# Strassen products in two-bank PSUM tiles, each moved by one operation over both halves, the last sum's copy in place

## The chip, the cores and the metric

The kernel runs on one core of one Trainium2 chip. The metric is the device time of one execution in microseconds. A core has a matrix engine (TensorE, PE in the profile, with PEld for its weight loads), VectorE (DVE), ScalarE (ACT), GpSimd (POOL) and SyncE (SP), each with its own queue of instructions, worked off in order. TensorE writes its results to PSUM, an accumulator memory of eight banks, each of 512 float32 columns on 128 partitions; VectorE and ScalarE read them from there into SBUF, the working memory. DMAs move data between SBUF and the main memory.

## The reference

One layer of a hybrid decoder for a prompt of 1024 tokens and 8 sample tokens, width 1024, all in float32:

```python
h = rmsnorm(x, norm_gain)
proj = h @ w_in
q, k, v, gla_g, a_lr, u, pool_g, xq, xg, merge = jnp.split(proj, split_pts, axis=-1)
...
br_gla = o * jax.nn.silu(gla_g)          # gated linear attention
br_pool = p * jax.nn.silu(pool_g)        # trailing-window means, a map per group
br_x = c * jax.nn.silu(xg)               # cross-attention into 256 memory tokens
branches = jnp.stack([br_gla, br_pool, br_x], axis=2)
bproj = jnp.einsum('btnw,nwd->btnd', branches, w_branch)
gates = jax.nn.sigmoid(merge.astype(jnp.float32)).reshape(B, T, N_BRANCH, D_MODEL)
merged = jnp.sum(gates * bproj.astype(jnp.float32), axis=2).astype(x.dtype)
y = merged @ w_out
return x + y, S.astype(x.dtype), new_hist
```

A final RMSNorm follows. The change touches the product `h @ w_in`: 1024 rows of weights by some 10000 columns, for 1032 tokens.

## The kernel before

**Precision.** A float32 product is made of three: each operand is split into a rounded part (hi, a copy on ScalarE) and the rest (lo, a subtraction on VectorE, both in `split`, lines 219 to 226), and `mm3` (239 to 243) issues hi by hi, hi by lo and lo by hi. So TensorE's work stands under lines 241, 242 and 243 whatever it computes.

**Strassen.** The input projection is cut into 40 pairs of 128 columns each (`pairs`, 325 to 334; numbered 0 to 39). For one pair the 2x2 block product of weights and tokens is made with seven products in place of eight (Winograd's form): 0 to 6, with the left operands a11, a12, s2, s1, s3, s4 and a22 and the right ones in `ops`. One product has 128 output rows and 516 token columns; they are computed in two halves of 258 columns (QT), c = 0 and 1, each in a PSUM bank of its own, each with 4 x 3 = 12 matmuls (`product`, 536 to 544). Partial sums are shared by accumulating in PSUM: the tile x takes products 0, 2, 4 and 6 in turn, y takes 1, z takes 3 and then 5. In between, a snapshot of x is copied to SBUF on ScalarE (`saved`, 551 to 554): r1 after product 0, r2 after 2, r3 after 4. VectorE makes the sums: y + r1 (line 611), z + r3 (628) and z + r2 (637); what x holds after product 6 is copied out as it is (645, with SiLU, or 647). These sums go to the tiles e1 and e2, get a SiLU in 12 of the pairs (28 to 39, the gated ones), and are stored by a DMA of POOL (`finish`, 565 to 587).

**Order on TensorE.** It is written out by hand, as is that of SyncE, which issues the loads. `seq` (337 to 342) puts product 0 of the next pair between products 4 and 5 of this one:

```python
    for i in range(NPAIR):
        seq += [(i, j) for j in range(1, 5)]
        if i + 1 < NPAIR:
            seq.append((i + 1, 0))
        seq += [(i, 5), (i, 6)]
```

Pair 39, the last, has no next one. After each half of a product, `fill` (1239 to 1246) may put a piece of other work on TensorE: the memory keys and values, cross-attention, the linear attention, the pooling, each as a stream of steps with costs that set when the next one is due. These use two PSUM banks, the tag pz. The Strassen tiles, the first transposes of the tokens (`quarter_transposed`), the branch projections (1411 to 1436) and the output projection (1461 to 1506) use six, the tag px.

**Order elsewhere.** On ScalarE, VectorE and POOL the order is made by a planner with a cost model, which follows the program's order where several instructions are ready. It hands out the slots of a tag too, and sets the waits: a matmul that writes a bank waits for the last operation that read it.

**Buffers that the change touches.** `PX` (96) gives one bank, six in all. `Q` (130) gives an SBUF tile of 258 columns, five in all, for r1, r2, r3 and, early on, for the results of the memory stage (`mkv`, 405 to 413), which two POOL DMAs each store (456 and 457).

Of the kernel before, what the change touches and what calls it, by code (L numbers as in the profile page):

```python
# [9 lines left out]
F32 = mybir.dt.float32  # L10
# [8 lines left out]
P = 128  # L19
# [7 lines left out]
DV = 256  # L27
# [20 lines left out]
def trunk_kernel(ctx: ExitStack, tc: tile.TileContext,  # L48
# [44 lines left out]
    ps = ctx.enter_context(tc.tile_pool(name="ps", bufs=1, space=bass.MemoryType.PSUM))  # L93
    ctx.enter_context(tc.manual_schedule(engines={nc.tensor.engine, nc.sync.engine}))

    def PX():
        return ps.tile([P, 512], F32, tag="px", name="px", bufs=6)

    def PZ():
        return ps.tile([P, 512], F32, tag="pz", name="pz", bufs=2)  # L100
# [27 lines left out]
        return wk.tile([P, 4, P], dt, tag="w2", name=name, bufs=8)  # L128

    def Q(name):  # L130
        return wk.tile([P, QT], F32, tag="q", name=name, bufs=5)

    def tiny(w, name="t", bufs=8):
        return wk.tile([P, 16], F32, tag="t", name=name, bufs=bufs)[:, :w]
# [255 lines left out]
    def mem_units():  # L390
        loads = [mem_weights(0)]
        yield
        loads.append(mem_weights(1))
        yield
        for n in range(NH):
            h, o = divmod(n, 2)
            raw = loads.pop(0)
            if 0 < n < NH - 1:
                loads.append(mem_weights(n + 1))
            for a in range(2):  # L400
                t = PZ()
                for k in range(NK):
                    nc.tensor.matmul(t[:, :DV], lhsT=memT[k // 2][:, k % 2, a * P:(a + 1) * P],  # L403
                                     rhs=raw[k // 2][:, k % 2], start=k == 0, stop=k == NK - 1)
                m = Q("mkv")[:, :DV]
                if n + a == 0:
                    nc.vector.tensor_copy(m, t[:, :DV])
                elif n == 0:
                    with tc.issue_after(last["sc"].ins):
                        nc.vector.tensor_copy(m, t[:, :DV])  # L410
                else:
                    nc.scalar.activation(m, t[:, :DV], AF.Copy)
                mem_stored(h, o, a, m)
                yield

        steps = [(o, k) for o in range(2) for k in range(NK)]
        ahead = []

        def stream():
            o, k = steps[len(ahead)]  # L420
            ahead.append(loaded((w_mk, w_mv)[o][k * P:(k + 1) * P, 512:], [512], "wms", V))

        memr = []
        memT_done.append(True)
        for k2, x in enumerate(memT):
            memr.append(split_r(x, [2, NM], "memT"))
            if k2 % 2:
                stream()
            if k2 == 1:
                yield  # L430
        parts = {k: split_r(ahead[k], [512], "wms") for k in range(2)}
        stream()
        yield
        for n, (o, k) in enumerate(steps):
            if k == 0:
                ts = [PZ() for _ in range(2)]
            if len(ahead) < len(steps):
                stream()
            if n + 2 < len(steps):
                parts[n + 2] = split_r(ahead[n + 2], [512], "wms")  # L440
            wh, wl = parts.pop(n)
            for a in range(2):
                mh, ml = (x[:, k % 2, a * P:(a + 1) * P] for x in memr[k // 2])
                mm3(ts[a], mh, ml, wh, wl, k == 0, k == NK - 1)
            if k == NK - 1:
                for a in range(2):
                    m = V([2, DV], name="mkv")
                    nc.scalar.activation(m, ts[a].rearrange("p (h v) -> p h v", h=2), AF.Copy)
                    for h in range(2):
                        mem_stored(2 + h, o, a, m[:, h])  # L450
                if o == 0:
                    yield
            yield
# [82 lines left out]
    def product(acc, n, start):  # L536
        i, j = seq[n]
        lh, ll = left[i, j]
        for c in range(2):
            for k in range(4):  # L540
                hi, lo = ops[RIGHT[j]][k // 2]
                rh, rl = (x[:, k % 2, c * QT:(c + 1) * QT] for x in (hi, lo))
                mm3(acc[c][:, :QT], lh[:, k, :], ll[:, k, :], rh, rl, start and k == 0, k == 3, not start)
            yield c

    def run_product(n):
# [1 line left out]
        i, j = seq[n]  # L548
        p = pairs[i]

        def saved(acc, c, name):
            r = Q(name)
            nc.scalar.activation(r, acc[c][:, :QT], AF.Copy)  # L553
            return r

        def piece(t, h, c):
            return t[:, h, c * QT:(c + 1) * QT]

        def diagonal(x, e):

# [28 lines left out]
        def gate(t, h):  # L589
            if p.gated:  # L590
                act(t[:, h], t[:, h], AF.Silu)
# [7 lines left out]
                    p.mix[e].append(loaded(mix_scr[n][g][:, ch, 512 * hf:512 * hf + 512], [512], "mix"))  # L599

        if j == 0:
            p.x = [PX() for _ in range(2)]
            p.r1, p.mix = [], ([], [])
            for c in product(p.x, n, True):
                p.r1.append(saved(p.x, c, "r1"))
                yield
        elif j == 1:
            y = [PX() for _ in range(2)]
            p.e1 = E([2, HT], name="c1")
            for c in product(y, n, True):  # L610
                nc.vector.tensor_tensor(piece(p.e1, 0, c), y[c][:, :QT], p.r1[c], op=ALU.add)
                if c:
                    gate(p.e1, 0)
                yield
        elif j == 2:
            p.r2 = []
            for c in product(p.x, n, False):
                p.r2.append(saved(p.x, c, "r2"))
                yield
        elif j == 3:  # L620
            p.z = [PX() for _ in range(2)]
            mixed(0)
            for c in product(p.z, n, True):
                yield
        elif j == 4:
            for c in product(p.x, n, False):
                r3 = saved(p.x, c, "r3")
                nc.vector.tensor_tensor(piece(p.e1, 1, c), p.z[c][:, :QT], r3, op=ALU.add)  # L628
                if c:
                    gate(p.e1, 1)  # L630
                    finish(p.e1, 0)
                yield
        elif j == 5:
            p.e2 = E([2, HT], name="c2")
            mixed(1)
            for c in product(p.z, n, False):
                nc.vector.tensor_tensor(piece(p.e2, 0, c), p.z[c][:, :QT], p.r2[c], op=ALU.add)
                if c:
                    gate(p.e2, 0)
                yield  # L640
        else:
            for c in product(p.x, n, False):
                dst = piece(p.e2, 1, c)
                if p.gated:
                    act(dst, p.x[c][:, :QT], AF.Silu)
                else:
                    nc.scalar.activation(dst, p.x[c][:, :QT], AF.Copy)
                if c:
                    finish(p.e2, 1)
                yield  # L650

# [745 lines left out]
    def w_out_unit(k, hf):  # L1397
# [10 lines left out]
        split(hi, lo, raw)  # L1408
        wo[k, hf] = hi, lo

    for u, (o, n, d) in enumerate(units):
        if d == 0 and o:
            br = [branch_k(n, k) for k in range(NK)]
        if u + 1 < len(units):
            fetch(u + 1)
        w, sig, acc = inputs.pop(u)
        act(sig, sig, AF.Sigmoid)
        ts = [PX() for _ in CH]
        for k in range(NK):
            lh, ll = (x[:, k % 4, :] for x in w[k // 4])  # L1420
            for t, (c0, cw) in zip(ts, CH):
                mm3(t[:, :cw], lh, ll, br[k][0][:, c0:c0 + cw], br[k][1][:, c0:c0 + cw], k == 0, k == NK - 1)
        for t, (c0, cw) in zip(ts, CH):
            cs = slice(c0, c0 + cw)
            nc.vector.tensor_tensor(sig[:, cs], t[:, :cw], sig[:, cs], op=ALU.mult)
            if o > 0:
                nc.vector.tensor_tensor(sig[:, cs], acc[:, cs], sig[:, cs], op=ALU.add)
        if o < 2:
            nc.gpsimd.dma_start(out=acc_scr[o][d], in_=sig)
        else:  # L1430
            if d < 5:
                mg_split(d, sig)
            else:
                late.append((d, sig))
            if d >= 2:
                w_out_unit(d - 2, 0)
# [29 lines left out]
            mm3(t[:, :b - a], th, tl, wh, wl, k == 0, k == NK - 1)  # L1466


    begun = [PX() for _ in range(2)]
    for ks in (range(5), range(5, NK)):  # L1470
        for tb in range(2):
            row_block(begun[tb], tb, 0, 0, 512, ks)
    for hf, order in enumerate(ORDERS):
        for tb in order:
            m = P if tb < 8 else NS
            if tb >= 8:

                if tb == 8:
                    ts = PX()
                for j in range(4):  # L1480
                    nc.tensor.matmul(ts[32 * j:32 * j + 32], lhsT=mgs[:, 4 * (tb - 8) + j], rhs=own.pop(0),
                                     start=tb == 8, stop=tb == 9)
                if 2 * hf + tb < 11:
                    own_weights(2 * hf + tb - 7)
                if tb == 8:
                    continue
                tb = 8
# [9 lines left out]
                nc.vector.tensor_tensor(yl[:, :512], x[:, :512], fg[:, :512], op=ALU.mult)  # L1497
            n, a = hf, 0
            for b in ends:
                t = ts if tb == 8 else begun.pop(0) if begun else PX()  # L1500
                cs = slice(512 * hf + a, 512 * hf + b)
                if tb < 8 and (hf or tb > 1):
                    row_block(t, tb, hf, a, b, range(NK))
# [57 lines left out]
```

## Time and profile before

| what | us |
| --- | --- |
| median of 3 runs | 1450.72 |
| lowest and highest | 1450.0 and 1452.0 |
| the profiled execution | 1452.08 |
| its span | 1450.2 |
| TensorE busy | 1421.7 |
| VectorE busy | 906.0 |
| ScalarE busy | 689.2 |
| GpSimd busy | 194.9 |

The span is the time from the first to the last instruction that the profile shows; the execution's own time has the launch around it. The granted TensorE clock was 0.999 of full speed. The 40 pairs fill the first three quarters (to about 1079 us), the branch projections the next part, the output projection the end. In rows of the trace, the numbers are the start in us, the duration in us, the engine, the line, the operation, the tile written, the tiles read, and the shapes; what stands in brackets is idle time of the engine before the instruction and what ended it. In rows of one line's instructions three durations in ns follow: the shortest, the median and the longest. In rows of stretches, the wall time comes first and then each engine's busy time, with its count.

### The profile page before, as it was taken

The page shows a single profiled execution, that of the slowest core. Times are in us where ns is not written, and L with a number is a line of the kernel's source. Part 1 is how long each engine was busy: PE and PEld are TensorE (multiplying, and loading weights), DVE is VectorE, ACT ScalarE, POOL GpSimd, SP SyncE. Part 2 cuts the span into 40 slices and gives each one's busy share as a digit, 9 for nine tenths or more (in the row PEclk, how much of TensorE's full clock was granted, in tenths as well). Part 3 has the DMA queues.
Part 4 walks back from the last instruction along what each step waited for, and adds up shares of the span by engine and source line. Part 5 has one row for each costly group of instructions (what it writes and reads, how often), then busy time and mean ns, then how long its engine had stood idle before and what let it go on. Part 6 is the DMA issues. An engine that isn't in the chain of part 4 may idle for free.

```text
span 1450.2 us, 28260 instructions
## 1 busy us (share of the span) xinstructions
PE 1421.7 (98%) x10753; PEld 1360.2 (94%) x10753; DVE 906.0 (62%) x2107; ACT 689.2 (48%) x1607; POOL 194.9 (13%) x353
## 2 busy tenths in 40 slices
PE   7999999998999999999999999999999999999998
PEld 6899999998899999999999999999999999999876
DVE  6956656666686767766756678785672434544436
ACT  6744435443465666656654445454472333233312
POOL 3112101124341111111111111110010000000000
PEclk9999999999999999999999999999999999999999
DMA  9346665666655453553544455455594677632633
GB/s 335 122 159 207 200 212 184 218 190 164 160 157 183 130 182 126 177 175 125 180 142 152 157 187 182 138 192 168 194 303 147 226 255 236 241 116 71 220 125 117
DMA packets 182739, 259.42 MB, mean 179 GB/s; under 512 B 21436, under 2 KB 131796, under 8 KB 182596
## 3 DMA queue, kind: packets, MB, share of 16 engines
q1 hardware_dynamic: 159900, 183.87, 41.4%
q0 software_dynamic: 22560, 73.56, 14.1%
q8 instruction: 84, 1.38, 0.4%
q14 instruction: 51, 0.42, 0.1%
q10 hardware_dynamic: 144, 0.20, 0.0%
HBM read 180.47 MB, written 77.56 MB: 178 GB/s over the span
## 4 chain that ended last, share of the span: by engine, by line
PE 86%; DMA 5%; DVE 5%; issue 2%; ACT 1%; SPq 0%; DVEq 0%; POOL 0%; ACTq 0%
PE px L241 25%; PE px L242 24%; PE px L243 24%; DMA qb<-xqs 2%; PE pz L243 2%; PE pz L242 2%; PE pz L241 2%; DMA raw<-in_w_in_dram 2%; DVE kc L769 1%; PE pz L403 1%; PE pz L955 1%; PE pz L936 1%; PE pz L809 1%; PE pz L938 1%; DVE ws L304 0%
## 5 line engine op out<-in xcount | busy, mean ns | idle before, releaser
L243 PE MATMUL px<-bh,wbl 128*128 128x384 f32 (+1 forms) x576 | 184.1, 320 | 0.0
L242 PE MATMUL px<-bl,wbh 128*128 128x384 f32 (+1 forms) x576 | 184.1, 320 | 0.0
L241 PE MATMUL px<-bh,wbh 128*128 128x384 f32 (+1 forms) x576 | 183.7, 319 | 0.0
L553 ACT ACTIVATE r<-px 128x258 f32<-128x258 f32 x240 | 90.0, 376 | 45.6 <-PE px L243 45.0
L241 PEld LDWEIGHTS px<-bh,wbh 128*128 128x128 f32 x576 | 108.3, 188 | 0.0
L242 PEld LDWEIGHTS px<-bl,wbh 128*128 128x128 f32 x576 | 108.2, 188 | 0.0
L243 PEld LDWEIGHTS px<-bh,wbl 128*128 128x128 f32 x576 | 108.2, 188 | 0.0
L241 PE MATMUL px<-ot,s1h 128*128 128x258 f32 x320 | 93.9, 293 | 0.0
L241 PE MATMUL px<-ot,s3h 128*128 128x258 f32 x320 | 93.4, 292 | 0.0
L241 PE MATMUL px<-o,s4h 128*128 128x258 f32 x320 | 93.2, 291 | 0.2 <-DVE c L628 0.2
L241 PE MATMUL px<-o,a11h 128*128 128x258 f32 x320 | 92.9, 290 | 0.0
L241 PE MATMUL px<-o,a12h 128*128 128x258 f32 x320 | 92.9, 290 | 0.0
L241 PE MATMUL px<-ot,a22h 128*128 128x258 f32 x320 | 92.9, 290 | 0.0
L241 PE MATMUL px<-ot,s2h 128*128 128x258 f32 x320 | 92.3, 288 | 0.0
L242 PE MATMUL px<-o,a11h 128*128 128x258 f32 x320 | 91.0, 284 | 0.3 <-DVE o L223 0.3
L243 PE MATMUL px<-o,a11l 128*128 128x258 f32 x320 | 90.6, 283 | 0.0
L242 PE MATMUL px<-ot,a22h 128*128 128x258 f32 x320 | 90.5, 283 | 0.0
L242 PE MATMUL px<-ot,s2h 128*128 128x258 f32 x320 | 90.0, 281 | 0.5 <-DVE ot L223 0.5
L243 PE MATMUL px<-ot,s3l 128*128 128x258 f32 x320 | 90.5, 283 | 0.0
L243 PE MATMUL px<-o,a12l 128*128 128x258 f32 x320 | 90.4, 283 | 0.0
L242 PE MATMUL px<-o,a12h 128*128 128x258 f32 x320 | 90.4, 283 | 0.0
L243 PE MATMUL px<-ot,s1l 128*128 128x258 f32 x320 | 90.4, 282 | 0.0
(470 smaller groups left out, 4616.0 us busy)
## 6 DMA issues: line engine op xcount, KB each, us to landing
raw<-in_w_in_dram SPq DMA_DIRECT2D x80, 512.0 KB, 4.0
msc<-c POOLq DMA_DIRECT2D x24, 516.0 KB, 4.3
brsc<-c POOLq DMA_DIRECT2D x24, 516.0 KB, 4.0
sig<-msc SPq DMA_DIRECT2D x24, 516.0 KB, 6.6
mix<-mixsc SPq DMA_DIRECT2D x48, 256.0 KB, 4.5
brr<-brsc SPq DMA_DIRECT2D x48, 256.0 KB, 5.2
wbr<-in_w_branch_dram SPq DMA_DIRECT2D x24, 512.0 KB, 6.1
acc<-sig POOLq DMA_DIRECT2D x16, 516.0 KB, 5.3
```

The source lines that it names most:

```text
L241: nc.tensor.matmul(out, lhsT=lh, rhs=rh, start=start, stop=False, skip_group_check=more)
L242: nc.tensor.matmul(out, lhsT=lh, rhs=rl, start=False, stop=False, skip_group_check=more)
L243: nc.tensor.matmul(out, lhsT=ll, rhs=rh, start=False, stop=stop, skip_group_check=more)
L403: nc.tensor.matmul(t[:, :DV], lhsT=memT[k // 2][:, k % 2, a * P:(a + 1) * P], rhs=raw[k // 2][:, k % 2], start=k == 0, stop=k == NK - 1)
L553: nc.scalar.activation(r, acc[c][:, :QT], AF.Copy)
L769: nc.vector.tensor_tensor_reduce(kc[:, a, :], kc[:, a, :], qb[:, bb, :], scale=1.0, scalar=0.0, op0=ALU.mult, op1=ALU.add, accum_out=sc[:, ...
L809: nc.tensor.matmul(t[32 * j:32 * j + 32, :DV], lhsT=pm[:, a, 4 * i + j, :], rhs=vc[j][:, a, :], start=a == 0, stop=a == 1)
L936: nc.tensor.matmul(t[0:64, 0:P], lhsT=ki[:, 0:64], rhs=qi, start=True, stop=True)
L938: nc.tensor.transpose(t[:, P:2 * P], kt, ident)
L955: nc.tensor.matmul(to, lhsT=kiqi[:, 1, cs], rhs=st, start=False, stop=True)
```

## The change

Each Strassen tile becomes one tile of two banks (`PX2`, three of them), and half c is accumulated in bank c as before. Copies and sums are no longer made per half: after the second half, one operation over both banks does it, with the two halves of 258 columns as a second dimension. The snapshots r1 and r2 get two-half slots, two in all, in place of five single ones. The third snapshot, r3, gets none: ScalarE writes it to the place in e1 where the sum will be, and VectorE adds z to it there. The product after which an operation is made, the matmuls and their order, and the DMAs are the same.

Users of single banks are adapted: `PX` hands out the halves of a two-bank tile in turn, the memory results take halves of a two-half slot (`MKV`), and the projections at the end take three two-bank tiles once and go round their six banks.

```diff
+    def PX2():
+        return ps.tile([P, 2, 512], F32, tag="px", name="px", bufs=3)
+
+    banks = []
+
     def PX():
-        return ps.tile([P, 512], F32, tag="px", name="px", bufs=6)
+        if not banks:
+            t = PX2()
+            banks.extend([t[:, 0], t[:, 1]])
+        return banks.pop(0)
+
+    def banks_of(ts):
+        while True:
+            yield from (t[:, i] for t in ts for i in range(2))
...
     def Q(name):
-        return wk.tile([P, QT], F32, tag="q", name=name, bufs=5)
+        return wk.tile([P, 2, QT], F32, tag="q", name=name, bufs=2)
+
+    halves = []
+
+    def MKV():
+        if not halves:
+            q = Q("mkv")
+            halves.extend(q[:, i, :DV] for i in range(2))
+        return halves.pop(0)
...
-                m = Q("mkv")[:, :DV]
+                m = MKV()
...
-                mm3(acc[c][:, :QT], lh[:, k, :], ll[:, k, :], rh, rl, start and k == 0, k == 3, not start)
+                mm3(acc[:, c, :QT], lh[:, k, :], ll[:, k, :], rh, rl, start and k == 0, k == 3, not start)
...
-        def saved(acc, c, name):
+        def saved(acc, name):
             r = Q(name)
-            nc.scalar.activation(r, acc[c][:, :QT], AF.Copy)
+            nc.scalar.activation(r, acc[:, :, :QT], AF.Copy)
             return r
 
-        def piece(t, h, c):
-            return t[:, h, c * QT:(c + 1) * QT]
+        def half(t, h):
+            return t[:, h].rearrange("p (c q) -> p c q", c=2)
...
             for c in product(p.x, n, True):
-                p.r1.append(saved(p.x, c, "r1"))
+                if c:
+                    p.r1 = saved(p.x, "r1")
                 yield
...
             for c in product(y, n, True):
-                nc.vector.tensor_tensor(piece(p.e1, 0, c), y[c][:, :QT], p.r1[c], op=ALU.add)
                 if c:
+                    nc.vector.tensor_tensor(half(p.e1, 0), y[:, :, :QT], p.r1, op=ALU.add)
                     gate(p.e1, 0)
                 yield
...
             for c in product(p.x, n, False):
-                r3 = saved(p.x, c, "r3")
-                nc.vector.tensor_tensor(piece(p.e1, 1, c), p.z[c][:, :QT], r3, op=ALU.add)
                 if c:
+                    nc.scalar.activation(half(p.e1, 1), p.x[:, :, :QT], AF.Copy)
+                    nc.vector.tensor_tensor(half(p.e1, 1), p.z[:, :, :QT], half(p.e1, 1), op=ALU.add)
                     gate(p.e1, 1)
                     finish(p.e1, 0)
                 yield
...
             for c in product(p.z, n, False):
-                nc.vector.tensor_tensor(piece(p.e2, 0, c), p.z[c][:, :QT], p.r2[c], op=ALU.add)
                 if c:
+                    nc.vector.tensor_tensor(half(p.e2, 0), p.z[:, :, :QT], p.r2, op=ALU.add)
                     gate(p.e2, 0)
                 yield
...
             for c in product(p.x, n, False):
-                dst = piece(p.e2, 1, c)
-                if p.gated:
-                    act(dst, p.x[c][:, :QT], AF.Silu)
-                else:
-                    nc.scalar.activation(dst, p.x[c][:, :QT], AF.Copy)
                 if c:
+                    if p.gated:
+                        act(half(p.e2, 1), p.x[:, :, :QT], AF.Silu)
+                    else:
+                        nc.scalar.activation(half(p.e2, 1), p.x[:, :, :QT], AF.Copy)
                     finish(p.e2, 1)
                 yield
...
+    bank = banks_of([PX2() for _ in range(3)])
...
-        ts = [PX() for _ in CH]
+        ts = [next(bank) for _ in CH]
...
-    begun = [PX() for _ in range(2)]
+    begun = [next(bank) for _ in range(2)]
```

Product 2's copy (r2) and the tiles x, y and z change in the same way as those shown; in the output projection each remaining `PX()` becomes `next(bank)`.

More of the change, by code (lines that the diff above doesn't have):

```diff
@@ L601, in run_product @@
         if j == 0:
-            p.x = [PX() for _ in range(2)]
-            p.r1, p.mix = [], ([], [])
+            p.x = PX2()
+            p.mix = ([], [])
             for c in product(p.x, n, True):
-                p.r1.append(saved(p.x, c, "r1"))
+                if c:
+                    p.r1 = saved(p.x, "r1")
                 yield
         elif j == 1:
-            y = [PX() for _ in range(2)]
+            y = PX2()
             p.e1 = E([2, HT], name="c1")
             for c in product(y, n, True):
-                nc.vector.tensor_tensor(piece(p.e1, 0, c), y[c][:, :QT], p.r1[c], op=ALU.add)
                 if c:
+                    nc.vector.tensor_tensor(half(p.e1, 0), y[:, :, :QT], p.r1, op=ALU.add)
                     gate(p.e1, 0)
@@ L615, in run_product @@
         elif j == 2:
-            p.r2 = []
             for c in product(p.x, n, False):
-                p.r2.append(saved(p.x, c, "r2"))
+                if c:
+                    p.r2 = saved(p.x, "r2")
                 yield
         elif j == 3:
-            p.z = [PX() for _ in range(2)]
+            p.z = PX2()
             mixed(0)
@@ L1478, in trunk_kernel @@
                 if tb == 8:
-                    ts = PX()
+                    ts = next(bank)
                 for j in range(4):
@@ L1499, in trunk_kernel @@
             for b in ends:
-                t = ts if tb == 8 else begun.pop(0) if begun else PX()
+                t = ts if tb == 8 else begun.pop(0) if begun else next(bank)
                 cs = slice(512 * hf + a, 512 * hf + b)
```

## The prediction

> **What bounds the kernel now.** I read the profile page first: which engine is busy, and where the chain of waits that ends last runs.
>
> ```profile
> PE 1421.7 (98%) x10753; PEld 1360.2 (94%) x10753; DVE 906.0 (62%) x2107; ACT 689.2 (48%) x1607; POOL 194.9 (13%) x353
> PE 86%; DMA 5%; DVE 5%; issue 2%; ACT 1%; SPq 0%; DVEq 0%; POOL 0%; ACTq 0%
> ```
>
> TensorE is busy for 1421.7 us of the 1450.2 us span and carries 86% of the chain. So work taken from ScalarE (ACT) or VectorE (DVE) pays only where TensorE stands still for it, and at most 28.5 us stand still in all. Next, the stretches (wall, then busy time per engine) and the waits of TensorE, to see where that is.
>
> ```profile
> 300.00:600.00 300.00, 291.66 (x2408) 276.81 (x2407) 207.66 (x545) 170.35 (x458) 72.87 (x120) 1.00 0.55 164
> 780.00:1000.00 220.00, 220.00 (x1844) 219.77 (x1844) 158.77 (x349) 104.70 (x223) 26.83 (x47) 1.00 0.52 167
> 1100.00:1400.00 300.00, 300.00 (x1813) 288.73 (x1812) 129.49 (x243) 89.97 (x150) 10.81 (x23) 1.00 0.57 187
> ```
>
> ```profile
> PE px L241 <- DVE c L628: 0.2, 1, 0.2
> ```
>
> From 780 us on there is nothing to win: 220.00 of 220.00 us busy, then 300.00 of 300.00. From 300 to 600 us 8.3 us are idle. And among the waits of TensorE, one alone is for the operations that the change merges: 0.2 us, once. The evacuations are hidden today. The question is whether they stay hidden when they start later and last longer.
>
> **What the merging saves.** These are the prices: the two ScalarE rows read PSUM with 258 and with 512 columns, and the two VectorE rows do the same.
>
> ```profile
> L553 ACT ACTIVATE r<-px x240: 358/370/417, 28.7 to 1072.4; 128x258 f32<-128x258 f32 x120
> L448 ACT ACTIVATE mkv<-pz x4: 591/598/599, 85.9 to 110.5; 128x512 f32<-128x512 f32 x4
> L628 DVE TENSOR_TENSOR c<-px,r x80: 400/420/429, 71.5 to 1073.1; 128x258 f32<-128x258 f32 x80
> L503 DVE TENSOR_TENSOR h<-px,vec x7: 669/680/693, 21.2 to 46.5; 128x512 f32<-128x512 f32 x7
> ```
>
> A 516-column operation is not in the trace. Its bounds are the 512-column row (0.598 and 0.680 us) and two 258-column ones (0.740 and 0.840 us); with the slope between the rows I take 0.60 us on ScalarE and 0.68 us on VectorE, the near end. Each of the 40 pairs has four ScalarE copies per half (products 0, 2, 4, 6) and three VectorE adds per half (1, 4, 5). So 320 copies become 160, at 2 x 0.370 - 0.60 = 0.14 us saved each, 22 us of ScalarE; 240 adds become 120, at 2 x 0.420 - 0.68 = 0.16 us each, 19 us of VectorE. That is 3% and 2% of what these engines do, none of it on the chain.
>
> What it gives TensorE is unknown. The bounds are 0 and the whole 8.3 us idle between 300 and 600 us; most of that idle time waits for DMAs and for long steps of the attention chain, and so lies near the low end. I take an eighth, -1.0 us.
>
> **What it delays: a pair in the steady state.** A merged operation can't start before the second half of its product is done, and its reader gives both banks back at once. The tightest case is product 4: copy on ScalarE, add on VectorE, and product 5 accumulates onto the same tile z, with one product (0 of the next pair) between. Here is pair 36: the last matmul of product 4, what ScalarE and VectorE do, the first matmul of product 5.
>
> ```profile
> 1011.27 0.28 PE L243 MATMUL px<-ot,s3l 128*128 128x258 f32 x1
> ...
> 1014.28 0.28 PE L241 MATMUL px<-o,s4h 128*128 128x258 f32 x1
> ```
>
> ```profile
> 1011.51 0.63 ACT L222 ACTIVATE a12h<-raw 128x512 fp32r<-128x512 f32 x1 [0.98 <-PE px L242]
> 1012.05 0.37 ACT L553 ACTIVATE r<-px 128x258 f32<-128x258 f32 x1
> ```
>
> ```profile
> 1012.18 0.69 DVE L223 TENSOR_TENSOR a12l<-raw,a12h 128x512 fp32r<-128x512 f32 x1 [1.19 <-ACT a12h L222]
> 1012.79 0.42 DVE L628 TENSOR_TENSOR c<-px,r 128x258 f32<-128x258 f32 x1
> ```
>
> The product ends at 1011.55. ScalarE first splits the next weights (a12h) and copies at 1012.05; merged, that copy ends at 1012.65. VectorE is at a12l until about 1012.8, so the add still starts at 1012.79 and ends at 1013.47. Product 5 starts at 1014.28: 0.8 us to spare, where before the half that came late (1013.21) was due only half a product (12 matmuls at a pitch of 0.12, 1.43 us) later, at 1015.71. Cost here nothing; the cover is the product between, 2.9 us. Where it is gone, the cost is the lateness itself. The same goes for product 2's copy (product 3 between it and product 4) and for product 5's add (product 6 before the next pair writes product 1, if the pool hands out the tile that came free first).
>
> **The last pair: no cover.** Pair 39 has no next pair, so product 5 follows product 4 at once.
>
> ```profile
> 1071.59 0.28 PE L243 MATMUL px<-ot,s3l 128*128 128x258 f32 x1
> 1071.71 0.39 PE L241 MATMUL px<-o,s4h 128*128 128x258 f32 x1
> ...
> 1073.13 0.28 PE L243 MATMUL px<-o,s4l 128*128 128x258 f32 x1
> 1073.60 0.39 PE L241 MATMUL px<-o,s4h 128*128 128x258 f32 x1 [0.18 <-DVE c L628]
> ```
>
> ```profile
> 1072.38 0.37 ACT L553 ACTIVATE r<-px 128x258 f32<-128x258 f32 x1
> ```
>
> ```profile
> 1073.12 0.42 DVE L628 TENSOR_TENSOR c<-px,r 128x258 f32<-128x258 f32 x1
> ```
>
> Today the second half waits a little: it comes at 1073.60 where the pitch would give 1073.13 + 0.12 = 1073.25. Merged, the copy runs 1072.38 to 1072.98, the add 1073.12 to 1073.80, and with 0.06 us from add to matmul (1073.54 to 1073.60 above) product 5 starts at 1073.86 instead of 1071.71: 2.15 us later. The 0.35 us of today falls away. Net +1.8 us. All of TensorE's later work is queued behind this matmul (product 6, the branch projections, the output projection), and the 300.00 busy of 300.00 us after it leave nowhere to make it good.
>
> A rule of the Trainium skill bears on that stall (PSUM — Partial Sum Buffer, section "PSUM bank collisions raise a hardware error"): no two engines may be in one bank at once, so the bank is guarded for an operation's whole length. If the first bank came free when the add is half through, the stall would be 0.34 us less, +1.5 us; by the rule it is the +1.8 us above. The rows before the change have one bank per operation and can't show which.
>
> **Pairs that are late for other reasons.** In some pairs the second half's copy or add stands behind an operation that waits. I looked at every pair for the time between the second half and the matmul that needs its tile; three stand out. Pair 9, product 5's add (352.74), and the matmul of pair 10 that would need the tile (349.06):
>
> ```profile
> 351.45 0.43 DVE L769 CUSTOM_DVE_ANT_0 kc<-kc,qb 128x256 f32<-128x256 f32 x1 [4.41 <-DMA qb<-xqs]
> ...
> 352.74 0.42 DVE L637 TENSOR_TENSOR c<-px,r 128x258 f32<-128x258 f32 x1
> ```
>
> ```profile
> 349.06 0.28 PE L241 MATMUL px<-o,a12h 128*128 128x258 f32 x1
> ...
> 352.54 0.39 PE L242 MATMUL pz<-pTl,mvsh 128*128 128x256 f32 x1 [1.76 <-DVE pTl L223]
> ...
> 356.85 0.33 PE L716 MATMUL pz<-ident,p 128*128 128x128 f32 x1 [1.08 <-ACT xo L728]
> ...
> 363.11 0.26 PE L795 MATMUL pz<-ident,ps 8*128 8x8 f32 x2 [2.74 <-DVE ps L790]
> ```
>
> The merged add would end at 353.42, 4.4 us after TensorE wants the tile. But TensorE waits anyway right after: 1.76 + 1.08 + 2.74 = 5.6 us, for a DMA (qb) and what it holds up. A stall that comes earlier takes the place of these. I take 0; the other end is +4.4.
>
> Pair 13, product 4's add (456.46) before product 5 (455.28), after a gap of ScalarE that the profile calls issue; and pair 5, product 2's copy (221.18) before product 4 (220.80):
>
> ```profile
> 450.07 0.51 ACT L1025 ACTIVATE s<-s,as 128x256 f32<-128x256 f32 x1 [3.38 <-issue]
> ```
>
> ```profile
> 456.46 0.42 DVE L628 TENSOR_TENSOR c<-px,r 128x258 f32<-128x258 f32 x1
> ```
>
> ```profile
> 455.28 0.47 PE L241 MATMUL px<-o,s4h 128*128 128x258 f32 x1
> ```
>
> ```profile
> 221.18 0.39 ACT L553 ACTIVATE r<-px 128x258 f32<-128x258 f32 x1
> ```
>
> ```profile
> 220.80 0.28 PE L241 MATMUL px<-ot,s3h 128*128 128x258 f32 x1
> ```
>
> Pair 13: 456.46 + 0.68 = 457.14, +1.9 us at most; the gap that causes it may fall elsewhere with fewer instructions on ScalarE, so I take a third, +0.6. Pair 5: 221.18 + 0.60 = 221.78, +1.0 us, taken whole.
>
> **What costs nothing.** The SBUF copies get two slots of two halves where five single ones were. r1 and r2 use one each in turn. The early memory keys share them: the slot that the first r2 copy will need is stored by DMAs, the last issued here, with the time that such a DMA takes to land below it,
>
> ```profile
> 51.46 0.54 POOL L457 DMA_DIRECT2D mkvs<-mkv  x1
> ```
>
> ```profile
> DMA to landing us min/median/max: 2.1/4.1/6.1
> ```
>
> and so it is free by 51.46 + 0.54 + 6.1 = 58.1 us at the latest, while that copy (its second half) ran here, on a ScalarE that would else be held with all splits queued behind it:
>
> ```profile
> 59.77 0.38 ACT L553 ACTIVATE r<-px 128x258 f32<-128x258 f32 x1
> ```
>
> The copy into the sum's own place (r3) needs no slot and has no earlier reader. The transposes take both halves of a tile in turn; a tile that comes back only when both are read can cost one 0.68 us evacuation, near the start, where VectorE's chain sets the pace: taken 0. The projections cycle through the same six banks. DMAs, their queues and their order on SP and POOL stay; what POOL stores comes at most 0.3 us later.
>
> **The sum.** +1.8 (pair 39) + 0.6 (pair 13) + 1.0 (pair 5) + 0 (pair 9) - 1.0 (relief) = +2.4 us. The profiled execution took 1452.08 us, 1.9 us over its span, and becomes 1454.5. It was 1.36 us above the median of the runs, 1450.72, which becomes 1453.1 us, 0.17% slower. About 0.2%, 2.9 us, is what a measurement of this kernel can tell from no change, so the likeliest verdict is no change that can be told.
>
> **The rivals.**
> - *Relief is large (faster).* The order on ScalarE and VectorE is planned anew. If the shorter lists let the attention chain of pair 9's stretch run ahead of the operation that waits for qb, the 5.6 us of waits there go. It decides once more than 1.8 + 2.9 = 4.7 us of idle time go. For it: two merged operations are two fewer points at which an engine queue stands for TensorE. Against it: the waits there start with a DMA. Time: 1450.7 + 1.8 - 5.6 - 1.0 = 1445.9. Chance 0.18.
> - *All lateness is paid.* The plan keeps each operation where its second half stands, and the stall of pair 9 delays the chain behind it too: 1.8 + 4.4 + 1.9 + 1.0 = +9.1, 1459.8 us. Against it: those waits have causes of their own. Chance 0.14.
> - *The pool hands product 1 the tile of product 6, not of product 5.* Then each pair waits for product 6's copy: 0.50 us of queue (1011.55 to 1012.05 above) and 0.60 us, 39 times, +43 us, 1494 us. Against it: product 5's tile comes free first. Chance 0.03.
> - *It does nothing on the path*: the planner puts pair 39's copy ahead and the rest cancels, 1450.7. Chance 0.05.
>
> The forecast has 0.60, with its own range of 1449.5 to 1456; of that 0.03 is faster, 0.36 within 0.2% and 0.21 slower. Summed: faster 0.03 + 0.18 = 0.21; within 0.36 + 0.05 = 0.41; slower 0.21 + 0.14 + 0.03 = 0.38. The range, 1447 to 1459, takes in most of both neighbours and leaves out their far ends.
>
> **What would show it.** Copies and adds of 128x516 at 0.60 and 0.68 us, 160 and 120 of them; one wait of TensorE for the add of product 4 (about 2 us) near 1072 us; in the steady pairs no wait for these operations; busy TensorE time from 780 us on as before, but for that. It is wrong if waits for merged operations show in many pairs, if the last pair doesn't stall, or if the idle time between 300 and 600 us changes by more than 4 us.

## The result, and the profile after

The changed kernel takes 1523.54 us (median of 4 runs, 1519.64 to 1529.1); the kernel before took 1451.36 us beside it. The ratio is 1.0501 with a 95% interval of 1.0467 to 1.0535: 72 us slower, where 2.4 us were forecast. The profiled execution took 1529.1 us with a span of 1527.4 us, 77.2 us over the span before.

From the page of the kernel after, busy time by engine and the granted clock in 40 slices:

```profile
PE 1452.4 (95%) x10753; PEld 1385.3 (91%) x10753; DVE 898.8 (59%) x1987; ACT 670.9 (44%) x1447; POOL 192.5 (13%) x353
PEclk8999999999999999999999999999999999999899
```

VectorE and ScalarE run 120 and 160 instructions fewer, as forecast; they are busy for 7.2 and 18.3 us less, where 19 and 22 were forecast. TensorE runs the same 10753 matmuls, but is busy for 30.7 us more (1452.4 against 1421.7) and idle for 46.5 us more (75.0 against 28.5). Both are losses, and they are of different kinds: idle is waiting, and longer busy time for the same work is a slower clock.

Where? First the kernel before, then the kernel after, in stretches: wall time, then busy time of TensorE, weight loads, VectorE, ScalarE and GpSimd, then the granted clock, the DMA share and GB/s. The cuts are the first 60 us, the start of the branch projections, and their end.

```profile
0.00:60.00 60.00, 51.91 (x341) 43.31 (x342) 44.54 (x92) 39.34 (x80) 17.60 (x49) 1.00 0.78 262
1078.00:1349.40 271.40, 271.40 (x1728) 271.40 (x1727) 118.61 (x231) 88.49 (x141) 12.43 (x25) 1.00 0.59 191
1349.40:1450.20 100.80, 94.38 (x444) 73.90 (x442) 47.45 (x108) 24.33 (x67) 0.19 (x1) 0.99 0.43 151
```

```profile
0.00:60.00 60.00, 48.76 (x257) 40.13 (x258) 35.98 (x82) 31.68 (x65) 15.11 (x44) 0.86 0.74 249
300.00:600.00 300.00, 291.68 (x2391) 278.33 (x2392) 204.30 (x504) 161.72 (x405) 72.79 (x122) 0.99 0.54 162
780.00:1000.00 220.00, 220.00 (x1844) 219.78 (x1843) 159.57 (x327) 99.97 (x184) 27.13 (x48) 1.00 0.52 168
1093.00:1405.60 312.60, 286.55 (x1728) 284.37 (x1727) 119.19 (x231) 87.75 (x138) 12.04 (x24) 0.96 0.49 164
1100.00:1400.00 300.00, 273.95 (x1648) 271.77 (x1648) 112.39 (x218) 80.49 (x127) 11.47 (x23) 0.95 0.48 160
1405.60:1527.40 121.80, 98.39 (x445) 75.17 (x443) 46.25 (x106) 23.57 (x66) 0.19 (x1) 0.94 0.34 121
```

The steady pairs are untouched: 220.00 of 220.00 us busy from 780 us on, as before. The branch projections take 312.6 us instead of 271.4 (+41.2), the output projection and the end 121.8 instead of 100.8 (+21.0), and the projections begin at 1093 us instead of 1078 (+15). In the first 60 us TensorE gets through 257 matmuls instead of 341, at a clock of 0.86. So 62 of the 77 us lie in a part whose arithmetic the change did not touch. TensorE's waits (total, times, longest) name what it waited for:

```profile
PE px L261 <- DVE sig L1446: 26.0, 12, 4.9
PE px L261 <- ACT px L1527: 15.4, 6, 7.6
PE px L513 <- ACT h L520: 4.9, 5, 1.2
PE px L261 <- DVE c L659: 4.3, 1, 4.3
PE px L261 <- DVE c L650: 3.1, 2, 1.9
```

Twelve of the 24 units of the branch projections wait for the VectorE that reads their blocks (L1446), 26.0 us in all; the output projection waits for L1527, ScalarE's last operation on its tiles (it sums squares and uses the tile that VectorE has read as scratch), 15.4 us; the transposes of the first 60 us wait for ScalarE's evacuation (L520), 4.9 us. Of these rows only the one for L650 stood among the waits before (there L628, 0.2 us, once). Only the last two rows, 7.4 us, belong to Strassen products, which the prediction was about.

One such unit, at 1206 us: the last matmul of the unit before and the first ones of the waiting unit, then VectorE.

```profile
1203.72 0.28 PE L263 MATMUL px<-bh,wbl 128*128 128x264 f32 x1
1206.12 0.41 PE L261 MATMUL px<-bh,wbh 128*128 128x384 f32 x1 [2.12 <-DVE sig L1446]
...
1206.87 0.53 PE L261 MATMUL px<-bh,wbh 128*128 128x384 f32 x1
```

```profile
1203.67 1.02 DVE L1446 TENSOR_TENSOR sig<-px,sig 128x384 f32<-128x384 f32 x2 [4.02 <-PE px L263]
1204.61 1.02 DVE L1448 TENSOR_TENSOR sig<-acc,sig 128x384 f32<-128x384 f32 x2
1205.55 0.43 DVE L1446 TENSOR_TENSOR sig<-px,sig 128x264 f32<-128x264 f32 x1
```

A unit uses three banks, so over six banks units alternate between the first three and the last three. Taken in pairs, the third bank of an even unit (its 264-column block) and the first bank of the odd unit after it are the two halves of one tile. The odd unit's first matmul goes into a bank that had been read a whole unit earlier, and still starts only when the read of the 264-column block is over (1205.55 + 0.43 = 1205.98): the reader of the other half. That read comes last of the three. Then the matmuls last 0.53 us where the same shape lasts 0.34 us in undisturbed units. The granted clock of the same place, and of a place that follows a shorter wait (1.35 us, at 1181 us), in stretches of after:

```profile
1203.00:1206.50 3.50, 1.38 (x9) 1.20 (x8) 2.30 (x5) 0.48 (x1) 0.00 (x0) 1.00 0.46 181
1206.50:1209.90 3.40, 3.40 (x14) 3.40 (x13) 1.04 (x2) 1.10 (x2) 0.53 (x1) 0.50 0.12 20
1209.90:1214.00 4.10, 4.10 (x28) 4.10 (x27) 0.00 (x0) 0.00 (x0) 0.00 (x0) 0.99 0.93 265
1181.20:1184.60 3.40, 3.40 (x22) 3.40 (x23) 1.62 (x4) 1.76 (x4) 0.53 (x1) 1.00 0.40 157
```

For 3.4 us after the wait the clock is 0.50: 12 matmuls start instead of 21 (the counts 14 and 22 take in those begun just before). Summed over the branch projections: matmul starts are late by 28.0 us in the twelve waits, and there are 27.3 us of stretches at 0.5, which cost at most half of that, 13.7 us; together 41.7 us, against 41.2 measured.

The theory from here on: **a two-bank tile is guarded as one thing**, so a matmul into one bank waits for the last operation on the other (A), and long waits cost a second time through the clock. The rival (B): the tiles are innocent, and the projections suffer from what the changed Strassen stage leaves behind (another order on ScalarE and VectorE, other arrival times).

### The profile page after: what moved, and what is told of

It is laid out like the page before. It is cut to its first block, busy times and chain, and to the rows that moved or that the text cites. A ratio compares the mean times of both kernels' runs of the same rounds, so it can differ in the third digit from the quotient of the medians.

```text
span 1527.4 us, 27981 instructions
## 1 busy us (share of the span) xinstructions
PE 1452.4 (95%) x10753; PEld 1385.3 (91%) x10753; DVE 898.8 (59%) x1987; ACT 670.9 (44%) x1447; POOL 192.5 (13%) x353
## 5 line engine op out<-in xcount | busy, mean ns | idle before, releaser
L261 PE MATMUL px<-bh,wbh 128*128 128x384 f32 (+1 forms) x576 | 190.5, 331 | 26.0 <-DVE sig L1446 26.0
L263 PE MATMUL px<-bh,wbl 128*128 128x384 f32 (+1 forms) x576 | 189.2, 328 | 0.0
L262 PE MATMUL px<-bl,wbh 128*128 128x384 f32 (+1 forms) x576 | 189.1, 328 | 0.0
L261 PEld LDWEIGHTS px<-bh,wbh 128*128 128x128 f32 x576 | 112.6, 195 | 28.2 <-issue 16.1
L262 PEld LDWEIGHTS px<-bl,wbh 128*128 128x128 f32 x576 | 112.9, 196 | 0.0
L263 PEld LDWEIGHTS px<-bh,wbl 128*128 128x128 f32 x576 | 112.5, 195 | 0.0
L261 PE MATMUL px<-o,s4h 128*128 128x258 f32 x320 | 93.8, 293 | 3.1 <-DVE c L650 3.1
L261 PE MATMUL px<-ot,s1h 128*128 128x258 f32 x320 | 94.2, 294 | 0.0
L261 PE MATMUL px<-ot,s2h 128*128 128x258 f32 x320 | 92.5, 289 | 0.0
L262 PE MATMUL px<-o,s4h 128*128 128x258 f32 x320 | 91.2, 285 | 0.0
L263 PE MATMUL px<-o,s4l 128*128 128x258 f32 x320 | 91.2, 285 | 0.0
L262 PE MATMUL px<-ot,s1h 128*128 128x258 f32 x320 | 90.6, 283 | 0.0
```

The costliest lines, as they stand in the source:

```text
L261: nc.tensor.matmul(out, lhsT=lh, rhs=rh, start=start, stop=False, skip_group_check=more)
L262: nc.tensor.matmul(out, lhsT=lh, rhs=rl, start=False, stop=False, skip_group_check=more)
L263: nc.tensor.matmul(out, lhsT=ll, rhs=rh, start=False, stop=stop, skip_group_check=more)
```

## The experiments

**Projections on one-bank tiles, the rest of the change kept (tail_single).** The Strassen stage has its three two-bank tiles in a pool that is closed ahead of the projections, which then get six one-bank tiles in its place.

```diff
+    early = ExitStack()
+    pe = early.enter_context(tc.tile_pool(name="pe", bufs=1, space=bass.MemoryType.PSUM))
...
-    bank = banks_of([PX2() for _ in range(3)])
+    early.close()
+    pl = ctx.enter_context(tc.tile_pool(name="pl", bufs=1, space=bass.MemoryType.PSUM))
+
+    def PX1():
+        return pl.tile([P, 512], F32, tag="px", name="px", bufs=6)
...
-        ts = [next(bank) for _ in CH]
+        ts = [PX1() for _ in CH]
```

> The changed kernel, but the branch and output projections work on six tiles of one bank each, as before the change; the Strassen stage and the first transposes keep two-bank tiles. Theory A (a two-bank tile is guarded as one: a matmul into one bank waits for the reader of the other, and the clock halves after the longer of these waits): the 41 us that the branch projections lost and the 21 us of the output projection come back, 1523.5 - 62 = 1461 us, with no wait of TensorE for the line that multiplies by the gate and a granted clock of 1.00 there. Theory B (the loss comes from the later, longer operations of the Strassen stage, and what is slow behind it follows from late operands or a clock that was lowered there): 1515 us or more.

Measured: 1469.5 us, ratio 1.0121 (1.0100 to 1.0143). The stretch of the projections that shows it:

```profile
1100.00:1400.00 300.00, 300.00 (x1844) 291.89 (x1843) 127.45 (x241) 92.24 (x148) 11.64 (x24) 1.00 0.58 191
```

300.00 of 300.00 us busy at full clock, as in the kernel before; the waits for L1446 and L1527 are gone, and with the waits the slow clock. The spans fall by 60.6 us (1527.4 to 1466.8), the medians by 54.0. A holds; B, with 1515 us or more, falls. 8.5 us remain over what A expected.

**The kernel before, projections alone on two-bank tiles (before_tail_pairs).** The other direction: nothing of the Strassen stage changes.

```diff
+    def banks_of(ts):
+        while True:
+            yield from (t[:, i] for t in ts for i in range(2))
...
+    bank = banks_of([pl.tile([P, 2, 512], F32, tag="px", name="px", bufs=3) for _ in range(3)])
...
-        ts = [PX() for _ in CH]
+        ts = [next(bank) for _ in CH]
```

> The kernel before, with one part of the change alone: the branch and output projections go round the six banks of three two-bank tiles. Every Strassen tile, copy and sum is as before. Theory A: 62 us slower, about 1513 us, with waits of TensorE for the other bank's reader at every second unit (1.4 to 2.3 us each). Theory B: 1451 us, since no Strassen operation is merged.

Measured: 1513.35 us, ratio 1.0423 (1.0402 to 1.0444), on A's 1513. Its waits:

```profile
PE px L247 <- DVE sig L1434: 26.8, 12, 4.9
PE px L247 <- ACT px L1515: 16.3, 6, 8.5
```

The same two rows as in the changed kernel (26.0 and 15.4 there), on top of an unchanged Strassen stage. Grouping the banks into tiles is sufficient for the 61 us, and the merged operations have no part in them.

**The shared bank last (shared_bank_last).** If the wait is for the other half of one tile, an odd unit that writes this half third instead of first should find it read already. In the changed kernel, odd units use their banks in rotated order, and every unit evacuates its third block first.

```diff
+        if u % 2:
+            ts = ts[1:] + ts[:1]
...
-        for t, (c0, cw) in zip(ts, CH):
+        for t, (c0, cw) in [(ts[i], CH[i]) for i in (2, 0, 1)]:
```

> The changed kernel with two-bank tiles everywhere, but in the branch projections the bank whose tile is shared with the unit before is written third (about 1 us after the unit's start) and the shared bank is read out first (0.42 us). Theory A: the wait at every second unit is over before its matmul comes, so the 41 us of the branch projections come back and the 21 us of the output projection stay: 1482 us. If the wait is for something else (slots, the order that the planner makes, late weights): still about 1523 us.

Measured: 1494.92 us, ratio 1.0296 (1.0259 to 1.0334). Its waits:

```profile
PE px L261 <- ACT px L1529: 18.3, 6, 10.5
PE px L261 <- DVE sig L1448: 4.6, 3, 2.5
```

The branch projections go from 26.0 us of waits to 4.6, three in place of twelve. The direction is A's; the gain is 29 us, not the 41 expected. In its profiled execution the branch projections take 279.4 us, 33 less than in the changed kernel, and 8 more than in the kernel before. The waits of the output projection, which this edit does not touch, grew from 15.4 to 18.3 us, and the longest of them from 7.6 to 10.5. That longest wait goes back to a load: the adds of the first row blocks (L1528) themselves wait 4.50 and 2.95 us for the DMA that brings their rows (y), and each square stands behind its add. In the changed kernel they wait 3.85 and 3.05 us. VectorE waits for these loads in the kernel before too (7.2 us at L1505), but there TensorE does not stand behind it.

**Filling the waits (warm).** Is the slow clock a consequence of TensorE standing still? In before_tail_pairs, dummy matmuls into a bank that nobody reads fill the place of each wait.

```diff
+        if u % 2:
+            warm = PZ()
+            for i in range(13 if o else 7):
+                nc.tensor.matmul(warm[:, :384], lhsT=br[0][0][:, :P], rhs=br[0][0][:, :384], start=True, stop=True)
```

> before_tail_pairs (the kernel before, projections alone on two-bank tiles) plus dummy matmuls of 128x384 into a PSUM bank that nobody reads, at the place in each odd unit at which TensorE waits for the reader of the other bank: 7 of them in the first branch, 13 later on. The output is unchanged. If the granted clock halves because TensorE sits still in those waits, the clock stays at 1.00 through the projections, the waits are filled with dummy work of about their own length, and the time is about 1513 - 12 = 1501 us. If the clock halves for another reason (how deep the work is queued, or the load), the half-clock windows stay and the time is 1513 us or more.

Measured: 1502.06 us, ratio 1.0352 (1.0324 to 1.0380). The same stretch, in before_tail_pairs first and with the dummy work second:

```profile
1100.00:1400.00 300.00, 274.41 (x1640) 270.54 (x1639) 117.56 (x225) 80.47 (x128) 10.80 (x23) 0.95 0.48 161
```

```profile
1100.00:1400.00 300.00, 297.07 (x1830) 290.47 (x1829) 121.05 (x230) 84.82 (x134) 10.84 (x23) 1.00 0.50 166
```

The dummy matmuls take about as long as the waits whose place they fill (two waits, 2.9 us in all, are left), yet the kernel gains 11 us (12 expected), because the clock is 1.00 instead of 0.95. The halved clock follows from standing still, and costs about 11 of the 61 us in the branch projections; the waits of the output projection were not filled.

**The transposes on unshared tiles (head_single).** In tail_single, the transposes of the first part take whole tiles of their own (a two-bank tile of which one bank is used, and a pz tile, in turn), so that no two of them share a tile.

```diff
-        if not banks:
-            t = PX2()
-            banks.extend([t[:, 0], t[:, 1]])
-        return banks.pop(0)
+        return PX2()[:, 0]
...
-            t = PX()
+            t = PZ() if k2 % 2 else PX()
```

> As the run with one-bank tiles in the projections, and in addition no tile of the first transposes is shared: each takes a whole slot or one of the two other banks in turn. Theory A: the waits for other banks' readers between 18 and 57 us go and the clock stays at 1.00 there; the 9 us by which the changed kernel was late at 190 us come back, about 1452 us, some 3.5 us of it the wait of the last pair with its slow clock. Theory B: no change against the run with one-bank tiles in the projections alone, 1461 us or whatever that gives.

Measured: 1464.92 us, ratio 1.0093 (1.0068 to 1.0117). The first 60 us of it:

```profile
0.00:60.00 60.00, 51.26 (x338) 42.54 (x339) 43.99 (x90) 38.65 (x78) 17.80 (x49) 1.00 0.78 262
```

338 matmuls at clock 1.00, nearly the 341 of before: the mechanism is right. But the whole kernel gains 4.6 us over tail_single, where 9 were expected to come back. The delay at the start is partly waited out later: in tail_single, the same matmuls lie 8.6 us behind the kernel before at 86 us, in head_single 0.0 us; at 750 us it is 11.5 against 6.7. What remains to be found is in the Strassen stage:

```profile
PE px L258 <- DVE c L647: 5.0, 3, 1.9
PE px L258 <- DVE c L656: 3.7, 1, 3.7
```

Three waits for product 4's add (L647), in pairs 2, 13 and 39, and the one of pair 9 for product 5's add (L656).

**The z tile read early (copy_z).** In head_single, e1 gets a copy of z right after product 3, and product 4 is added to it from PSUM by VectorE. Product 5 then finds its tile z free.

```diff
             for c in product(p.z, n, True):
+                if c:
+                    nc.scalar.activation(half(p.e1, 1), p.z[:, :, :QT], AF.Copy)
                 yield
...
-                    nc.scalar.activation(half(p.e1, 1), p.x[:, :, :QT], AF.Copy)
-                    nc.vector.tensor_tensor(half(p.e1, 1), p.z[:, :, :QT], half(p.e1, 1), op=ALU.add)
+                    nc.vector.tensor_tensor(half(p.e1, 1), p.x[:, :, :QT], half(p.e1, 1), op=ALU.add)
```

> head_single with one step of the sums turned round: z is copied to the second half of e1 by ScalarE as soon as product 3 has been added, and VectorE adds product 4 straight from its PSUM tile to that copy, where head_single copies product 4 and adds z to it. The z tile is free long before product 5 wants it. Theory: the rest of head_single over the kernel before is TensorE waiting for the late product-4 additions (1.68 us at 146, 1.88 us at 460, 2.09 us at 1081 us and the 3.4 us at half clock that follow it). Then these three waits and the half-clock window after 1081 us are gone: 1464.9 - 1.7 - 1.9 - 2.1 - 1.7 = about 1457.5 us. Rival: the planner puts the new copies where other evacuations then come late, and the time stays at 1465 us or goes above it.

Measured: 1459.77 us, ratio 1.0064 (1.0040 to 1.0088). Three waits that are longer than in the kernel before, or that it does not have:

```profile
PE pz L258 <- DVE pTl L240: 4.0, 1, 4.0
PE px L258 <- DVE c L657: 3.3, 1, 3.3
PE px L258 <- ACT c L75: 2.2, 1, 2.2
```

The waits for product 4's add are gone. Others grew over head_single: the one for an attention split at 294 us (pTl) from 1.6 to 4.0 us, and the one at 1088 us, where the projections' first matmul waits for product 6's merged copy (L75), from 0.7 to 2.2. Theory and rival both hold in part; the median is 2.3 us above what the theory expected, and its interval overlaps that of head_single.

**The last pair's products 5 and 6 exchanged (last_pair_swapped).** The last pair alone, in head_single: product 6 stands between product 4's add and product 5. Its weights are prepared, and its sums stored, in that order too (not shown).

```diff
-        seq += [(i, 5), (i, 6)]
+        seq += [(i, 5), (i, 6)] if i + 1 < NPAIR else [(i, 6), (i, 5)]
```

> head_single with products 5 and 6 of the last pair alone in exchanged order, so that the late product-4 addition is wanted one product later. Theory: the wait of 2.09 us at 1081 us shrinks below 1.4 us and no half-clock window follows it: 1464.9 - 1 - 1.7 = about 1462 us. Rival: the wait only moves to the other tile: 1465 us.

Measured: 1462.59 us, ratio 1.0077 (1.0059 to 1.0096). The end of the Strassen stage, head_single first, this kernel second:

```profile
1080.00:1100.00 20.00, 18.48 (x117) 18.28 (x118) 8.14 (x18) 13.52 (x19) 1.28 (x2) 0.91 0.90 287
```

```profile
1080.00:1100.00 20.00, 18.31 (x127) 18.14 (x126) 9.29 (x20) 14.32 (x21) 1.82 (x3) 1.00 0.86 274
```

The wait of 2.1 us became two: one of 1.2 us ahead of product 6, for the copy of product 4, and one of 1.8 us ahead of the projections, for the add of product 5. Neither is followed by a slow stretch: 127 matmuls in place of 117. The trace shows the mechanism; the difference of the times (1.0093 and 1.0077) lies within the intervals.

No version beats the kernel before. The best, copy_z, is 9 us above it. A part of that is visible (the wait of pair 9, the two waits that grew, stretches at half clock beside all three); how much each is worth at the end of the kernel was not separated, and stays open.

## Why the prediction was wrong, step by step

**The step that failed** is in "What costs nothing": "The projections cycle through the same six banks." They do, but not as the same six tiles. It was priced at 0 and measured 61 us, alone (before_tail_pairs), of a change worth 72. The prediction asked of a tile how long its reader takes; it did not ask which other matmuls share the tile's guard. The rows for it were there: projections busy for 300.00 of 300.00 us, so any wait there is paid in full, and blocks of three in tiles of two.

**"The transposes ... taken 0"** failed in the same way. It named the mechanism ("a tile that comes back only when both are read") and put its price at one evacuation of 0.68 us at most; five waits came to 4.9 us, and the clock fell to 0.86 over the first 60 us. By head_single it is worth 4.6 us at the end.

**A second price for each wait was missing.** All terms counted a stall at its own length. A stall of 2 us could be followed by 3.4 us at half clock, 1.7 us more, and of the 61 us that the projections lost alone, 11 came that way in the branch projections (warm).

**Prices of the merged operations: right, one by one.** From the groups of lines of the kernel after (busy time, mean ns of one):

```profile
L573 ACT ACTIVATE r<-px 128x516 f32<-128x516 f32 x80 | 46.8, 585 | 0.4 <-PE px L263 0.3
L659 DVE TENSOR_TENSOR c<-px,r 128x516 f32<-128x516 f32 x40 | 27.7, 692 | 22.1 <-PE px L263 21.8 <-issue 0.2
```

0.585 and 0.692 us, against 0.60 and 0.68; the counts are as forecast. The 19 us that the prices gave for VectorE did not all show in its busy time (7.2 us). It cost nothing, since these engines are not the limit.

**Steady pairs: right.** The waits for L650 and L659 are three in 40 pairs, and none of the three lies in the stretch from 780 to 1000 us.

**The last pair: right in its wait, short by the clock.** Forecast, product 5 is 2.15 us late. In the kernel after:

```profile
1085.00 0.69 DVE L650 TENSOR_TENSOR c<-px,c 128x516 f32<-128x516 f32 x1
```

```profile
1085.74 0.39 PE L261 MATMUL px<-o,s4h 128*128 128x258 f32 x1 [1.93 <-DVE c L650]
```

The add ends at 1085.69, the matmul starts at 1085.74, 2.09 us later than its pitch would give. But 3.4 us at half clock follow, so that over the last pair the lag behind the kernel before grows from 11.9 to 15.1 us: +3.2 where +1.8 stood. On the question whether the bank comes free when the operation is half through, nothing was learned: the program itself waits for the operation's end.

**Pair 9: right.** The wait is 4.3 us, 4.4 were worked out, and the later waits took it up: the lag is 10.8 us ahead of it and 9.4 us after (at 346 and 382 us of the kernel before), although 6.8 us at half clock stand beside it. TensorE's idle time from 300 to 600 us is 8.32 us, as against 8.34 before.

**Pair 13** has the other wait for L650, 3.1 - 1.9 = 1.2 us, where 0.6 was taken between 0 and 1.9. **Pair 5**, +1.0 in the sum, shows no wait. **The relief**, -1.0, shows nowhere: the idle time between 300 and 600 us, from which it was to come, did not shrink. So the sum's terms inside the Strassen stage were off by a microsecond or two each, and the forecast's miss of 70 us is almost all in the steps priced at zero. The rival that the pool would hand out another tile (1494 us) came nearest in size, and by another mechanism.

## What to carry to other kernels

When tiles become larger, list everyone who takes one, not only the operations that the change is for: a wait goes by the tile, so two users who share one wait for each other's readers. Look first at the stretch in which the bottleneck engine is 100% busy, for there each new wait is paid in full, and may be paid again through the clock, however little of the change seems to be in it. And a term of zero deserves the question of what it would cost if wrong: here one sentence carried 61 us.

## What the runs showed of the hardware

The granted clock of TensorE falls to half for 3.4, 6.8 or 10.2 us at a time (the kernel's end cuts the last stretch short), and the length of a wait does not say alone whether it will. Measured by how late the next matmul starts, the waits ahead of the odd units of the kernel after were of four sizes: those of 1.35 us (three) were never followed by half clock, those of 2.28 us in five cases of seven, those of 2.9 and 5.0 us both times. In the output projection, five waits of 1.6 us brought none.

The traces show what decides. In every profile that has more than one, the starts of the stretches at half clock lie whole steps of 3.413 us apart: in the kernel after, all thirteen of them, from 22.11 to 1523.97 us. The clock falls at such a border when TensorE was busy for less than about half of the step before it. Here are two waits of the same length, 2.12 us of idle time each: the step before the border and the step behind it, first for the wait that ends at 1206.12 us, then for the one that ends at 1341.38 us.

```profile
1203.12:1206.53 3.41, 1.29 (x8) 1.11 (x8) 2.30 (x5) 0.51 (x1) 0.00 (x0) 1.00 0.43 169
1206.53:1209.94 3.41, 3.41 (x14) 3.41 (x13) 1.04 (x2) 1.07 (x2) 0.53 (x1) 0.50 0.12 21
1339.65:1343.06 3.41, 1.68 (x11) 1.71 (x12) 3.13 (x7) 1.02 (x2) 0.53 (x1) 1.00 0.00 0
1343.06:1346.48 3.42, 3.42 (x23) 3.42 (x23) 1.93 (x2) 1.75 (x3) 0.00 (x0) 1.00 0.73 200
```

The first wait lies within one step, which leaves 1.29 of 3.41 us busy, and the clock halves. A border at 1339.65 us cuts the second in two; 1.68 us are busy, and the clock stays. Over the nine profiles, 47 steps fell from full clock to half, each after a step with a busy share of 0.49 or less. Of some 3770 steps that stayed at full clock, three followed a share below that (0.45 to 0.47; the first 10 us of each profile are left out). The first 60 us fit: after the first 5 us no single wait there was over 1.3 us, but many lie close together, and the shares before 22.1 and 52.8 us, where 10.2 and 6.8 us at half clock begin, were 0.44 and 0.46.

The Trainium skill (TensorE: Matmul & The Clock Gate, section "HAM oscillation — how this bites in real kernels") says that idle gaps of more than about 3.4 us make the clock fall back, and that the cost is half of the throttled time. The second part agrees (28.0 us of waits and half of 27.3 us come to 41.7, where 41.2 were measured); the first is too generous here, since 2.12 us idle at 1206 us sufficed, and the measurement decides. The section after it on the same page ("A second HAM failure mode: psum-queue depth-cycling") tells of frequent short idling between groups of matmuls that makes the clock swing. The first 60 us, with their many short waits, look like that.
